# A SwiGLU layer's up passes: the products of the lower right weight blocks, gate and up together, by seven products of half blocks instead of two whole ones

## The chip, the cores and the metric

The kernel runs on one core of one Trainium2 chip. The metric is the device time of one execution in microseconds (us). Before the change it is 2227.25 us, the median of 3 runs (2226.83 to 2227.45).

## What is computed

The reference is one decoder layer in float32: x has 1024 tokens of 1024 features.

```python
x = x + 0.5 * swiglu(rms_norm(x, ffn1_norm), ffn1_w_gate, ffn1_w_up, ffn1_w_down)
h = rms_norm(x, mix_norm)
...                                   # two attentions, gates, output projection
x = x + 0.5 * swiglu(rms_norm(x, ffn2_norm), ffn2_w_gate, ffn2_w_up, ffn2_w_down)
x = x + sigmoid(rms_norm(x, ple_norm) @ w_ple_gate) * (p @ w_ple_proj)

def swiglu(h, w_gate, w_up, w_down):
    return (silu(h @ w_gate) * (h @ w_up)) @ w_down
```

The change lies in the two `swiglu` calls, in `h @ w_gate` and `h @ w_up`: 1024 tokens by 1024 features by 2816 hidden units, each.

## The kernel before

**Products of one block.** The hidden units of gate and up are taken in 22 blocks of 256: block n is a gate block if n is even and an up block if n is odd, so that n = 2j and n = 2j+1 belong together. A block is a product of a 256 x 1024 weight matrix with the 1024 x 1024 activations. `ffn` (L400) does it by a scheme with seven block products in place of eight: both matrices are cut in four, sums of quarters are formed, and seven products of a 128 x 512 weight part with a 512 x 512 part of the activations are added up in four results. They are numbered 1 to 7 in the code. Each number is worked out three times with float32r operands, split in a high part and the rest (high by high, rest by high, high by rest), four slices of 128 deep: 12 matmuls of 128x512, recorded at L584 in `product`. Product 4 is the lower right weight quarter, `part(n, 4)`, against `B[4]`.

**Leaf products.** For products with the same right hand side, the weight parts of two neighbouring blocks can be laid on each other and the scheme can be used once more, at half the size: two products of 128 x 512 by 512 x 512 become seven of 128 x 256 by 256 x 256. The kernel does so for product 2 (`B[2]`) of the blocks n-1 and n, for odd n from 7 to 19. `inner_product` (L525) is one such half product: 6 matmuls of 128x256, recorded at L544, and one addition of the result to the block's sum in SBUF by VectorE (L548; 128x256, one input in PSUM, one in SBUF). The sums of weight halves are made by `inner_sums` (four VectorE additions, L506 to L509, both inputs in SBUF), the sums of the activations once per FFN by `inner_operands`, and kept in four tiles (G, WH, KH, KL) for all blocks.

**Operands.** `prep(n, m)` (L561) makes the left operand of one product: ScalarE copies the high part (L112, a cast), VectorE subtracts for the rest (L113). It stands four steps ahead of the product (`LA = 4`). `sums(n)` makes the sums of a block's weights and `last_sum` another one, both on GpSimd (L475 to L477, L480). `load` fetches a block's weights, two transfers on SyncE's queue, which all transfers share.

**Results.** `evict` moves results out of PSUM: copies on ScalarE (L602, L604, L606), additions on VectorE (L607, L611), SiLU on ScalarE (L614, L616), the products of gate and up on VectorE (L622, L624, L627). Product 4 of a gate block is read from PSUM by the SiLU (L616), that of an up block by the multiplication (L624). `hidden_sums` then forms sums of finished blocks on GpSimd (`block_sums`, L281: four additions, L283 to L286), which go to DRAM for the down product.

**Order.** The order is written out by hand: `seqn` lists the steps (block, product) in the order of TensorE, `seqp` the order in which operands are made. Each engine works through its own queue in the order in which the code records it; a queue does not pass a waiting instruction. A string as product, as in `(n, "65")`, stands for half products.

Of the kernel before, what the change touches and what calls it, by code (L numbers as in the profile page):

```python
# [38 lines left out]
def tile_hybrid_decoder_layer(  # L39
# [131 lines left out]
    fd = dp.tile([NH, S], F32, name="forget_sums")  # L171
    ad = [dp.tile([NF, P, 7, 512], F32, name=f"hidden_{i}") for i in range(2)]
# [227 lines left out]
    def ffn(N, wg, wu, wd, next_gain, resid, hid, tags, entry, tail):  # L400
# [12 lines left out]
        inner = range(6, nm_ - 2)  # L413
        for n in range(4, nm_ - 1):
            if n not in inner:
                steps = [(n, 1), (n - 1, 4), (n, 2), (n - 1, 3), (n, 6), (n, 5), (n, 7)]
                ahead = steps
            elif n % 2 == 0:
                steps = [(n, 1), (n - 1, 4), (n - 1, 3), (n, 6), (n, 5), (n, 7)]
                ahead = steps  # L420
            else:
                steps = [(n, 1), (n - 1, 4), (n, "12"), (n - 1, 3), (n, "65"), (n, 6), (n, "7"), (n, 5), (n, "3"), (n, 7), (n, "4")]
                ahead = [(n, 1), (n, "12"), (n - 1, 4), (n, "65"), (n - 1, 3), (n, 6), (n, "73"), (n, 5), (n, 7), (n, "4"), None]
            seqn += steps
            seqp += ahead
        n = nm_ - 1
        steps = [(n, 1), (n - 1, 4), (n, 2), (n, 6), (n, 5), (n, 7), (n - 1, 3), (n, 3), (n, 4)]
# [5 lines left out]
        turns = {"hl": 0, "t": 0}  # L433
# [18 lines left out]
        def plain(f_, half, parts=(0, 1), out=True):  # L452
# [5 lines left out]
            for kh in parts:  # L458
                hl, rb = hls[0, ((1, 2), (5, 4))[f_][kh]], B[("12", 3)[kh]] if half else N[0]["B"][kh]
# [22 lines left out]
        I = {}  # L482

        def inner_operands(step):

            x_ = I["x"] if step else I.setdefault("x", [slot(t, [P, 2, 512]) for t in ("GF", "RN")])
            a, b = slice(0, 256), slice(256, 512)
            if step < 2:
                nc.vector.tensor_add(x_[step][:], f(pair(2, 0, step)), f(pair(2, 1, step)))
            elif step == 2:  # L490
                nc.vector.tensor_sub(x_[0][:, :, a], x_[0][:, :, b], x_[0][:, :, a])
                nc.vector.tensor_sub(x_[0][:, :, b], x_[1][:, :, b], x_[0][:, :, b])
            elif step == 3:
                nc.vector.tensor_sub(x_[1][:, :, b], x_[1][:, :, b], x_[0][:, :, a])
                nc.vector.tensor_sub(x_[1][:, :, a], x_[1][:, :, a], x_[1][:, :, b])
            else:
                i = step - 4
                t = I[i] = [slot(t, [P, 2, 512], F32R) for t in (("G", "WH"), ("KH", "KL"))[i]]
                split(t[0][:], t[1][:], x_[i][:], nc.scalar, nc.vector)

        def inner_sums(n):

            s = I["s"] = slot("GF", [P, 4, 2, P])
            g, u = part(n - 1, 2), part(n, 2)
# [6 lines left out]
        def inner_prep(n, q):  # L511
            if q == "12":
                inner_sums(n)
                of = part(n - 1, 2)
            elif q == "4":
                of = part(n, 2)[:, 2:4]
# [4 lines left out]
            tag = "RN" if q == "73" else hl_tag()  # L521
            hl = slot(tag, [P, 2, nk, P], F32R)
            split(hl[:, 0], hl[:, 1], of, nc.scalar, nc.vector)
            for i, c in enumerate(q):
                I[c] = hl[:, :, 2 * i:2 * i + 2, :]  # L525
            if q == "12":
                last_sum(n - 1)
            elif q == "4":
                last_sum(n)

        def inner_product(n, c):

# [1290 lines left out]
```

## Time and profile before

| | before |
|---|---|
| median of 3 runs | 2227.25 us |
| the profiled execution | 2226.93 us |
| its span, first to last instruction | 2225.2 us |
| TensorE busy | 2211.6 us, 99% |
| VectorE busy | 1606.7 us, 72% |
| ScalarE busy | 983.6 us, 44% |
| GpSimd busy | 829.0 us, 37% |
| TensorE clock granted | 1.00 |
| first and last half product (L544) | at 163.0 and at 1877.1 us |

The profile is one execution recorded by the hardware. A row of a grouped view names line, engine, operation, output and inputs, then count, busy time, mean duration of one in ns, and the idle time in front of it with what ended it. A matmul's recorded duration overlaps with the next, so the pace of TensorE is read from the starts, not from the duration. The chain of waits is followed back from the last instruction; where it stays on one engine, that engine never waited.

### The profile page before, as it was taken

How to read it: one execution, taken by the hardware profiler on the slowest of the kernel's cores; microseconds unless marked ns; L12 is line 12 of the kernel's file. 1: busy time of each engine (PE TensorE's matmuls, PEld its weight loads, DVE VectorE, ACT ScalarE, POOL GpSimd, SP SyncE). 2: the span in 40 equal slices, each digit the busy share in tenths (PEclk: the TensorE clock that was granted, in tenths of full speed). 3: DMA queues.
4: the chain of work that ended last, by engine and by line, in shares of the span. 5: the costliest groups of instructions: out<-in, count | busy, mean ns of one | idle time of the engine just before them, and what ended most of it. 6: DMA issues, size and time to landing. Idle time of an engine off the chain costs nothing.

```text
span 2225.2 us, 29609 instructions
## 1 busy us (share of the span) xinstructions
PE 2211.6 (99%) x10949; PEld 1860.4 (84%) x10949; DVE 1606.7 (72%) x2390; ACT 983.6 (44%) x1726; POOL 829.0 (37%) x709
## 2 busy tenths in 40 slices
PE   9999999999999999999999999999999999999999
PEld 7888888888889888888988888887888888888887
DVE  7976667597895565666667676799876766778873
ACT  6433333333454555555456564255333333434441
POOL 0344545310015466455456654400644535200111
PEclk9999999999999999999999999999999999999999
DMA  8232323374433133042124246741423332756132
GB/s 323 92 121 88 117 89 123 138 295 145 148 132 94 31 95 93 24 104 72 38 72 119 62 128 213 263 142 54 142 101 103 105 109 92 259 192 211 59 120 89
DMA packets 187713, 278.06 MB, mean 125 GB/s; under 512 B 27944, under 2 KB 110120, under 8 KB 187568
## 3 DMA queue, kind: packets, MB, share of 16 engines
q1 hardware_dynamic: 187568, 276.17, 37.5%
q8 instruction: 86, 1.41, 0.3%
q14 instruction: 59, 0.48, 0.1%
HBM read 192.47 MB, written 75.27 MB: 120 GB/s over the span
## 4 chain that ended last, share of the span: by engine, by line
PE 90%; DVE 5%; ACT 3%; issue 1%; DMA 1%; POOL 0%; SPq 0%; ACTq 0%; DVEq 0%; POOLq 0%
PE ps L584 32%; PE ps L388 19%; PE ps L857 10%; PE ps L849 7%; PE ps L1759 4%; PE ps L1404 3%; PE ps L544 3%; PE ps L1160 3%; PE ps L1136 2%; PE ps L462 2%; PE ps L1085 1%; PE ps L1084 1%; PE ps L1454 1%; DVE H L113 1%; DVE RN L1060 1%
## 5 line engine op out<-in xcount | busy, mean ns | idle before, releaser
L388 PE MATMUL ps<-H,H 128*128 128x512 f32 x2184 | 497.2, 389 | 0.0
L388 PEld LDWEIGHTS ps<-H,H 128*128 128x128 f32 x2184 | 409.5, 188 | 84.8
L584 PE MATMUL ps<-H,WL 128*128 128x512 f32 x816 | 194.7, 390 | 0.0
L584 PEld LDWEIGHTS ps<-H,WL 128*128 128x128 f32 x816 | 151.8, 188 | 30.6
L857 PE MATMUL ps<-H,WH 128*128 128x512 f32 x640 | 175.9, 401 | 0.0
L1139 DVE TENSOR_TENSOR PT<-ps,PT 128x512 fp32r<-128x512 f32 (+1 forms) x160 | 100.6, 634 | 73.2 <-ACT PT L1138 72.2
L396 DVE SCALAR_TENSOR_TENSOR X<-ps,X 128x512 f32<-128x512 f32 x168 | 108.7, 685 | 41.8 <-PE ps L388 41.7
L584 PE MATMUL ps<-H,Q 128*128 128x512 f32 x552 | 132.8, 390 | 0.0
L857 PEld LDWEIGHTS ps<-H,WH 128*128 128x128 f32 x640 | 113.9, 188 | 19.0
L1138 ACT CAST PT<-ps 128x512 fp32r<-128x512 f32 (+1 forms) x160 | 86.9, 549 | 83.5 <-PE ps L1136 79.4
L146 POOL TENSOR_TENSOR WL<-RAW,WH 128x512 fp32r<-128x512 f32 (+1 forms) x92 | 109.1, 1206 | 38.6 <-ACT WH L136 33.0
L584 PE MATMUL ps<-X,WL 128*128 128x512 f32 x504 | 121.5, 390 | 0.0
L584 PEld LDWEIGHTS ps<-H,Q 128*128 128x128 f32 x552 | 102.4, 188 | 20.4
L480 POOL TENSOR_TENSOR KL<-KL,RAW 128x512 f32<-128x512 f32 x20 | 26.1, 1303 | 242.4 <-DVE Q L113 100.2
L209 POOL TENSOR_TENSOR PT<-PT,RN 128x1024 f32<-128x1024 f32 x2 | 4.8, 2402 | 295.1 <-ACT RN L203 295.1
L849 PE MATMUL ps<-WH,H 128*128 128x256 f32 (+2 forms) x576 | 111.4, 323 | 0.1
L584 PEld LDWEIGHTS ps<-X,WL 128*128 128x128 f32 x504 | 93.9, 188 | 19.6 <-DVE WL L113 0.5
L1097 POOL TENSOR_TENSOR T<-T,l 128x128 f32<-128x128 f32 (+3 forms) x64 | 73.1, 1148 | 88.7 <-DVE l L1096 84.7
L1160 PE MATMUL ps<-PT,X 128*128 128x256 f32 (+1 forms) x480 | 101.2, 315 | 3.9 <-DVE PT L1139 2.3
L1160 PEld LDWEIGHTS ps<-PT,X 128*128 128x128 f32 x480 | 76.7, 189 | 22.7 <-DVE PT L1139 9.7
L1107 POOL TENSOR_TENSOR T<-T,RN 128x383 f32<-128x383 f32 (+2 forms) x64 | 77.1, 1205 | 46.0 <-DVE RN L1060 43.7
L1060 DVE TENSOR_TENSOR_SCAN RN<-GF,RN 128x127 f32<-128x127 f32 (+2 forms) x96 | 91.1, 949 | 2.7
(468 smaller groups left out, 5116.9 us busy)
## 6 DMA issues: line engine op xcount, KB each, us to landing
hidden<-PT SPq DMA_DIRECT2D x40, 512.0 KB, 2.9
WH<-in_ffn_w_gate_dram SPq DMA_DIRECT2D x38, 512.0 KB, 4.3
Q<-hidden SPq DMA_DIRECT2D x24, 512.0 KB, 6.8
hidden<-RN SPq DMA_DIRECT2D x22, 512.0 KB, 2.6
KH<-in_ffn_w_up_dram SPq DMA_DIRECT2D x20, 512.0 KB, 3.8
KL<-in_ffn_w_up_dram SPq DMA_DIRECT2D x20, 512.0 KB, 3.8
T<-in_ffn_w_down_dram SPq DMA_DIRECT2D x20, 512.0 KB, 4.6
RAW<-in_w_in_dram SPq DMA_DIRECT2D x18, 512.0 KB, 4.3
```

Source lines behind the costliest of these rows:

```text
L146: ins = eng_lo.tensor_sub(lo[part], raw[part], f(hi[part]))
L388: pe(nc.tensor.matmul(groups[g][t][:], wt[:, b, k, t * P:(t + 1) * P], act[:, a, k, :], start=(fresh and n == 0), stop=(i in (6, 1, 4) and ...
L396: nc.vector.scalar_tensor_tensor(xs, groups[g][t][:], scale, xs, ALU.mult, ALU.add)
L584: pe(nc.tensor.matmul(ps[:], hl[:, a, k, :], rhs(m, b, k), start=(first and i == 0), stop=(final and i == 11), skip_group_check=True))
L849: pe(nc.tensor.matmul(ps[:, :n], hT[t // 4][a][:, k, (t % 4) * P:(t % 4 + 1) * P], w[k // d][b][:, k % d, :n], start=(i == 0), stop=(i == ...
L857: pe(nc.tensor.matmul(ps[:], w[a][:, k, :], hT[half][b][:, k, :], start=(i == 0), stop=(i == 23)))
L1060: order("dve", nc.vector.tensor_tensor_scan(*args))
L1107: nc.gpsimd.tensor_mul(T[:, cut:n - 1], T[:, cut:n - 1], R[:, cut:n - 1])
L1138: high = nc.scalar.copy(pt[:, 0, :width], ps[:, :width])
L1139: low = nc.vector.tensor_sub(pt[:, 1, :width], ps[:, :width], f(pt[:, 0, :width]))
L1160: pe(nc.tensor.matmul(o, lh, r, start=(kpair == c and i == 0), stop=(kpair == 0 and i == len(mm) - 1)))
L1759: pe(nc.tensor.matmul(ps, pl["w"][d, k // 2][b][:, k % 2, m * P:(m + 1) * P], hT[half][a][:, k, cs], start=(i == 0), stop=(i == 23)))
```

## The change

Product 4 of two neighbouring blocks is now done by seven half products too, in pairs that are shifted by one: an up block n-1 and the next gate block n, for even n from 8 to 20. So `inner` holds all n from 7 to 20; odd n take `part(.., 2)` and `B[2]`, even n `part(.., 4)` and `B[4]` (`leaf_of`).

- In each of the two FFNs 14 whole products (12 matmuls of 128x512 each) go, and 7 x 7 half products (6 matmuls of 128x256 each) come. The steps of a pair of blocks are reordered, and `seqp` is now the same as `seqn`.
- The half products of a gate block add to E[n][1] after ScalarE has copied product 7 there as well (L679, a second copy); the SiLU of that half (L598) and the product of gate and up (L601) read SBUF, behind these additions, and no longer PSUM.
- The sums of the activations are needed twice now and do not fit. `inner_tile` makes four tiles for each of the two; those of half product 5 stay in SBUF, those of 6, 7 and 4 are written to DRAM (6 transfers of 512 KB per FFN) and fetched again for each use (`inner_load`, 42 transfers of 512 KB per FFN, two tiles ahead, in one KL and one WH buffer that alternate).
- Buffers for left operands are handed out from a list of free ones (`hl_slot`).
- The block sums on GpSimd of a finished pair now follow the step `(n, "34")` of an even n.

Line numbers shift: what is L548 before is L594 after, L550 is L596, L616 L598 (in SBUF) or L689, L624 L601 (in SBUF) or L697, L607 L680, L611 L684, L480 L489, L283 to L286 L284 to L287.

The core of the diff:

```diff
-        inner = range(6, nm_ - 2)
+        inner = [n for n in range(6, nm_ - 1) if n > 6 and (n % 2 == 0 or n < nm_ - 2)]
+        by_inner = {2: [m for n in inner if n % 2 for m in (n - 1, n)], 4: [m for n in inner if n % 2 == 0 for m in (n - 1, n)]}
         for n in range(4, nm_ - 1):
...
+            steps = [(n, 1)]
+            if n - 1 in inner and n % 2:
+                steps.append((n - 1, "34"))
...
+            elif n % 2:
+                steps += [(n, "65"), (n, 6), (n, "7"), (n, 5), (n, 7), (n, "34")]
             else:
...
+                steps += [(n, "6"), (n, 6), (n, 5), (n, 7), (n, "57")]
             seqn += steps
-            seqp += ahead
+            seqp += steps
...
+        def inner_tile(leaf, c):
+
+            i, cs = {"5": (0, 0), "7": (0, 256), "4": (1, 0), "6": (1, 256)}[c]
+            t = slot("WH" if c != "5" else ("G", "KH")[leaf // 4], [P, 2, 2, 256], F32R)
+            split(t[:, 0], t[:, 1], I["x"][i][:, :, cs:cs + 256], nc.scalar, nc.vector)
+            if c == "5":
+                TT[leaf, c] = t
+            else:
+                nc.sync.dma_start(td[leaf, c], f(t[:]))
...
+        def inner_load():
+
+            n, c = stream[turns["s"]]
+            t = TT[n, c] = slot(("KL", "WH")[turns["s"] % 2], [P, 2, 2, 256], F32R)
+            nc.sync.dma_start(f(t[:]), td[leaf_of(n), c])
+            turns["s"] += 1
...
+            nc.vector.tensor_add(to, to, ps)
+            if m == 2 and c == "3":
+                nc.scalar.activation(x1[:], x1[:], AF.Silu)
+            elif m == 4 and c == "4":
+                nc.scalar.activation(y1[:, 0, :], y1[:, 0, :], AF.Silu)
+            elif m == 4 and c == "3":
+                g2 = E[n - 2][1]
+                nc.vector.tensor_mul(g2[:, 0, :], g2[:, 0, :], x1[:, 0, :])
+                nc.sync.dma_start(hid[(n - 2) // 2, :, 1:3, :], g2[:])
+            if c in "674" and turns["s"] < len(stream):
+                inner_load()
...
+        INNER_AT = {x_: (2 + 2 * (i // 6), i % 6) for i, x_ in enumerate(((4, 1), (3, 4), (4, 2), (3, 3), (4, 6), (4, 7), (5, 1), (4, 4), (5, 2), (4, 3), (5, 6), (5, 7)))}
...
             elif m == 7:
                 nc.scalar.copy(e2[:, 1, :], ps[:])
+                if n in by_inner[4]:
+                    nc.scalar.copy(e2[:, 0, :], ps[:])
...
+                if n % 2 == 0 and n in inner and m == "34":
+                    hidden_sums(n - 1, ("PT", "PT"))
+                elif n % 2 and m == (4 if n == 1 else 3) and n < nm_ - 1 and n not in by_inner[4]:
                     hidden_sums(n, ("PT", "PT"))
```

The steps of a pair of blocks, an even n and the odd n+1, in TensorE's order, before: (n, 1), (n-1, 4), (n-1, 3), (n, 6), (n, 5), (n, 7), (n+1, 1), (n, 4), (n+1, "12"), (n, 3), (n+1, "65"), (n+1, 6), (n+1, "7"), (n+1, 5), (n+1, "3"), (n+1, 7), (n+1, "4"). After: (n, 1), (n, "12"), (n-1, 3), (n, "6"), (n, 6), (n, 5), (n, 7), (n, "57"), (n+1, 1), (n, "34"), (n+1, "12"), (n, 3), (n+1, "65"), (n+1, 6), (n+1, "7"), (n+1, 5), (n+1, 7), (n+1, "34").

Three places show what moves on the engines beside TensorE. In these rows a number behind a tile's name is its buffer's; GF and RN hold the two halves of a gate block, Y those of an up block, PT the sums of finished blocks, WL, Q and PT left operands.

The first is ScalarE and VectorE in an up block, around the SiLU of the gate's second half. ScalarE before:

```order
L614 ACTIVATE RN_1519<-RN_1519 128x512
L112 CAST WL_1624<-GF_1584 128x512
L602 COPY Y_1640<-ps_1627 128x512
L112 CAST WL_1643<-WH_1347 128x512
L616 ACTIVATE RN_1519<-ps_1505 128x512
L112 CAST Q_1663<-RAW_1556 128x512
```

ScalarE after:

```order
L687 ACTIVATE RN_1929<-RN_1929 128x512
L112 CAST WL_2040<-WH_1712 128x512
L112 CAST Q_2060<-WH_1712 128x512
L673 COPY Y_2080<-ps_2067 128x512
L112 CAST Q_2083<-GF_2035 128x512
L598 ACTIVATE RN_1929<-RN_1929 128x512
L112 CAST PT_2105<-RAW_1996 128x512
```

The SiLU of one half of RN (L616, L598) reads PSUM before and SBUF after; behind it on the queue stands the high part of the up block's product 6 (Q_1663 before, PT_2105 after). VectorE at the same place, from the operand of "12" on, before:

```order
L113 TENSOR_TENSOR PT_1589<-WH_1347,PT_1589 128x512
L113 TENSOR_TENSOR WL_1606<-WH_1347,WL_1606 128x512
L607 TENSOR_TENSOR RN_1519<-RN_1519,ps_1593 128x512
L113 TENSOR_TENSOR WL_1624<-GF_1584,WL_1624 128x512
L113 TENSOR_TENSOR WL_1643<-WH_1347,WL_1643 128x512
L113 TENSOR_TENSOR Q_1663<-RAW_1556,Q_1663 128x512
```

VectorE after:

```order
L113 TENSOR_TENSOR WL_2040<-WH_1712,WL_2040 128x512
L594 TENSOR_TENSOR RN_1929<-RN_1929,ps_1942 128x256
L594 TENSOR_TENSOR RN_1929<-RN_1929,ps_1934 128x256
L113 TENSOR_TENSOR Q_2060<-WH_1712,Q_2060 128x512
L113 TENSOR_TENSOR Q_2083<-GF_2035,Q_2083 128x512
L594 TENSOR_TENSOR Y_1729<-Y_1729,ps_1942 128x256
L601 TENSOR_TENSOR RN_1577<-RN_1577,Y_1729 128x512
L594 TENSOR_TENSOR RN_1929<-RN_1929,ps_1934 128x256
L113 TENSOR_TENSOR PT_2105<-RAW_1996,PT_2105 128x512
```

The last addition to RN_1929, which the SiLU of L598 reads, stands behind two operands (Q_2060, Q_2083) and the product of gate and up of the blocks before (L601). `inner_sums` of the up block stand ahead of the first row.

The second is GpSimd in the same pair of blocks. Before:

```order
L283 TENSOR_TENSOR PT_1863<-GF_1518,RN_1519 128x512
L284 TENSOR_TENSOR PT_1863<-PT_1863,GF_1518 128x512
L285 TENSOR_TENSOR PT_1864<-GF_1518 128x512
L286 TENSOR_TENSOR PT_1864<-RN_1519,PT_1863 128x512
L480 TENSOR_TENSOR WH_1647<-WH_1647,RAW_1755 128x4x128
L480 TENSOR_TENSOR KL_1792<-KL_1792,RAW_1856 128x4x128
```

After:

```order
L489 TENSOR_TENSOR WH_1712<-WH_1712,RAW_1844 128x4x128
L284 TENSOR_TENSOR PT_2108<-GF_1576,RN_1577 128x512
L285 TENSOR_TENSOR PT_2108<-PT_2108,GF_1576 128x512
L286 TENSOR_TENSOR PT_2109<-GF_1576 128x512
L287 TENSOR_TENSOR PT_2109<-RN_1577,PT_2108 128x512
L489 TENSOR_TENSOR KL_1892<-KL_1892,RAW_1996 128x4x128
```

The four sums of finished blocks stood ahead of the gate's last sum (WH) and stand behind it now.

The third is ScalarE at the turn from an up block to the next gate block, around the SiLU of the tile GF (both halves, 128x1024). Before:

```order
L550 ACTIVATE GF_1518<-GF_1518 128x1024
L112 CAST WL_1770<-KL_1492 128x512
L606 COPY Y_1641<-ps_1627 128x512
L112 CAST Q_1788<-KL_1492 128x512
L112 CAST Q_1802<-RAW_1755 128x512
```

After:

```order
L112 CAST WL_2240<-KL_1892 128x512
L596 ACTIVATE GF_1928<-GF_1928 128x1024
L112 CAST WL_2264<-GF_2216 128x512
L673 COPY GF_2280<-ps_2267 128x512
L112 CAST WL_2283<-RAW_2196 128x512
```

The cast behind the SiLU was one of a whole product's operand (WL_1770, product 4) and is now that of half product "6" of the gate block (WL_2264).

More of the change, by code (lines that the diff above doesn't have):

```diff
@@ L171, in tile_hybrid_decoder_layer @@
     fd = dp.tile([NH, S], F32, name="forget_sums")
+    td_ = [dp.tile([P, 2, 2, 256], F32, name=f"inner_{i}") for i in range(12)]
     ad = [dp.tile([NF, P, 7, 512], F32, name=f"hidden_{i}") for i in range(2)]
@@ L432, in ffn @@
         W, hls, E = {}, {}, {}
-        turns = {"hl": 0, "t": 0}
+        turns = {"hl": 0, "t": 0, "s": 0}
         def cyc(key, tags):
@@ L458, in plain @@
             for kh in parts:
-                hl, rb = hls[0, ((1, 2), (5, 4))[f_][kh]], B[("12", 3)[kh]] if half else N[0]["B"][kh]
+                hl, rb = hls[0, ((1, 2), (5, 4))[f_][kh]][0], B[("12", 3)[kh]] if half else N[0]["B"][kh]
                 for a, b in ((0, 0), (1, 0), (0, 1)):
@@ L496, in inner_operands, with leaf_of @@
             else:
-                i = step - 4
-                t = I[i] = [slot(t, [P, 2, 512], F32R) for t in (("G", "WH"), ("KH", "KL"))[i]]
-                split(t[0][:], t[1][:], x_[i][:], nc.scalar, nc.vector)
+                inner_tile(leaf, "6574"[step - 2])
+                if step == 5:
+                    del I["x"]
+        stream = [(n, c) for n in inner for c in "674"]
+        def inner_load():
[3 more added lines that the diff above has]
+            turns["s"] += 1
+        def leaf_of(n):
+            return 2 if n % 2 else 4
         def inner_sums(n):
+            m = leaf_of(n)
             s = I["s"] = slot("GF", [P, 4, 2, P])
-            g, u = part(n - 1, 2), part(n, 2)
+            g, u = part(n - 1, m), part(n, m)
             lo, hi = slice(0, 2), slice(2, 4)
@@ L545, in inner_product, with hl_slot @@
                     i += 1
-            g1, u1 = E[n - 1][0], E[n][0]
-            for to in {"1": (g1[:, 0, a],), "2": (g1[:, 0, a],), "6": (g1[:, 0, b],), "5": (u1[:, 0, b],), "7": (u1[:, 0, b],), "3": (g1[:, 0, b],), "4": (u1[:, 0, a],)}[c]:
-                nc.vector.tensor_add(to, to, ps)
-            if c == "3":
-                nc.scalar.activation(g1[:], g1[:], AF.Silu)
-        def hl_tag():
+            uses[0] -= 1
+            if uses[0] == 0:
+                free.append(uses[1])
+            x1, y1 = (E[k][m // 4] for k in (n - 1, n))
+            to = {"1": x1[:, 0, a], "2": x1[:, 0, a], "6": x1[:, 0, b], "5": y1[:, 0, b], "7": y1[:, 0, b], "3": x1[:, 0, b], "4": y1[:, 0, a]}[c]
+            nc.vector.tensor_add(to, to, ps)
[9 more added lines that the diff above has]
+                inner_load()
+        free = []
+        def hl_slot(nk=4):
             k = turns["hl"]
             turns["hl"] += 1
-            return tags["hl"][k] if k < len(tags["hl"]) else ("WL", "WL", "WL", "Q", "Q", "PT")[k % 6]
+            if k < len(tags["hl"]):
+                tag = tags["hl"][k]
+            else:
+                if k == len(tags["hl"]):
+                    held = [t for (i, _), (_, t) in hls.items() if i]
+                    for t in ("WL", "WL", "WL", "Q", "Q", "PT"):
+                        if t in held:
+                            held.remove(t)
+                        else:
+                            free.append(t)
+                    assert not held, held
+                tag = free.pop(0)
+            return slot(tag, [P, 2, nk, P], F32R), tag
         def prep(n, m):
@@ L563, in prep @@
                     last_sum(n)
-            hl = hls[n, m] = slot(hl_tag(), [P, 2, 4, P], F32R)
+            hls[n, m] = hl_slot()
+            hl = hls[n, m][0]
             split(hl[:, 0], hl[:, 1], part(n, m), nc.scalar, nc.vector)
@@ L579, in product @@
             first, final = m in (1, 2, 5), m in (4, 2, 3)
-            hl = hls.pop((n, m))
+            hl, tag = hls.pop((n, m))
+            if turns["hl"] > len(tags["hl"]):
+                free.append(tag)
             i = 0
@@ L616, in evict @@
                     nc.scalar.activation(e2[:, 0, :], ps[:], AF.Silu)
-                elif m == 3 and n not in inner:
+                elif m == 3 and n not in by_inner[2]:
                     nc.scalar.activation(e1[:], e1[:], AF.Silu)
```

74 lines of the change are left out of this document (43 added, 31 removed).

## The prediction

> **What bounds the kernel now.** First the page's busy times, then what TensorE waited for (the waits, TensorE alone), then three pairs of blocks as windows, then the chain of waits inside one pair.
>
> ```profile
> PE 2211.6 (99%) x10949; PEld 1860.4 (84%) x10949; DVE 1606.7 (72%) x2390; ACT 983.6 (44%) x1726; POOL 829.0 (37%) x709
> ...
> PE ps L1160 <- DVE PT L1139: 2.3, 9, 0.5
> ...
> PE ps L584 <- DVE PT L113: 0.2, 1, 0.2
> ```
>
> TensorE is busy 99% of the span; its longest kind of wait is 2.3 us in all, and the whole products (L584) waited 0.2 us once. TensorE is the bound, and everything else is hidden behind it.
>
> ```profile
> core 0: us, PE busy (x) PEld busy (x) DVE busy (x) ACT busy (x) POOL busy (x), PEclk, DMA share, GB/s
> ...
> 238.99:276.77 37.78, 37.78 (x188) 32.05 (x188) 25.62 (x34) 13.78 (x25) 17.74 (x12) 1.00 0.32 105
> ...
> 201.21 1.43 PE ps L544 x12
> 202.64 2.75 PE ps L584 x12
> 205.39 1.43 PE ps L544 x12
> 206.82 2.75 PE ps L584 x12
> 209.57 0.71 PE ps L544 x6
> ...
> 217.20 21.79 PE ps L584 x96
> 238.99 1.43 PE ps L544 x12
> ```
>
> A pair of blocks takes 37.78 us, all of it TensorE, at the full clock; VectorE works 25.6 us of it in 34 instructions, GpSimd 17.7. The chain stays on TensorE and gives its prices: a whole matmul 21.79/96 = 0.2270 us (a product 2.72), one of a half product 1.43/12 = 0.1192, and about 0.03 each time that whole products follow halves (2.75 against 2.72).
>
> **TensorE's own gain.** Per FFN 14 whole products of 12 go: 2 x 14 x 12 = 336 matmuls, 336 x 0.2270 = 76.3 us. 2 x 49 half products of 6 come: 588 x 0.1192 = 70.1 us. Runs of halves go from 5 to 7 per pair, 28 more changes at 0.03, 0.8 us. Together -5.4 us: seven half-size products for two whole ones (eight halves' worth) save little here because a half matmul costs 0.525 of a whole one. With the row 0.71/6 in place of 1.43/12 the term is -5.9.
>
> [...]
>
> So the whole gain is a quarter of a per cent, 0.4 us per pair, and it is there only if the other engines stay hidden. I count a change within 0.2% (4.5 us) as none, about what a measurement of this kernel can tell.
>
> **What VectorE gets.** Its prices, from the groups of the three pairs:
>
> ```profile
> L548 DVE TENSOR_TENSOR GF<-GF,ps 128x256 f32<-128x256 f32 x12 | 5.0, 418 | 3.0 <-PE ps L544 2.7
> L506 DVE TENSOR_TENSOR GF<-WH,KL 128x256 f32<-128x256 f32 x3 | 4.5, 1514 | 0.0
> ...
> L622 DVE TENSOR_TENSOR RN<-RN,Y 128x512 f32<-128x512 f32 x3 | 3.2, 1075 | 0.1
> L624 DVE TENSOR_TENSOR RN<-RN,ps 128x512 f32<-128x512 f32 x3 | 2.1, 688 | 2.7 <-PE ps L584 2.7
> ...
> L113 DVE TENSOR_TENSOR Q<-KH,Q 128x512 fp32r<-128x512 f32 x3 | 2.0, 683 | 0.0
> ...
> L480 POOL TENSOR_TENSOR KL<-KL,RAW 128x512 f32<-128x512 f32 x3 | 3.9, 1286 | 37.6 <-DVE WL L113 25.1 <-DVE Q L113 12.5
> ```
>
> Per pair come 7 additions of half products (7 x 0.42 = 2.9 us), one and a half operands (1.0) and 4 sums of weight halves; the product L624 becomes one with both inputs in SBUF (0 to 0.4 more). The sums are the open price: no row shows one undisturbed, so 0.42 us (as L548, the same size) is the low end and 1.51 (L506) the high end, 1.7 to 6.1 us for four. VectorE goes from 25.6 us to between 31.2 and 36.0 of a pair that should take 37.4. On average it still fits. It works in order, though, so what counts is whether each operand is ready when TensorE comes to it.
>
> L506 costs 1.51 us because GpSimd is adding at the same time:
>
> ```profile
> 211.03 1.28 POOL L480 TENSOR_TENSOR KL<-KL,RAW 128x512 f32<-128x512 f32 x1 [12.53 <-DVE WL L113]
> 211.20 1.67 DVE L113 TENSOR_TENSOR WL<-WH,WL 128x512 fp32r<-128x512 f32 x1
> 212.28 1.74 POOL L475 TENSOR_TENSOR RAW<-WH 128x512 f32<-128x512 f32 x1
> ...
> 227.73 1.62 POOL L283 TENSOR_TENSOR PT<-GF,RN 128x512 f32<-128x512 f32 x1 [1.22 <-issue]
> 228.12 1.51 DVE L506 TENSOR_TENSOR GF<-WH,KL 128x256 f32<-128x256 f32 x1
> ```
>
> A VectorE operation with both inputs in SBUF that starts during a GpSimd addition ends 0.56 us after it (212.87 against 212.31), and the next GpSimd addition ends 1.15 us after that (214.02): the two take turns, 1.7 us a turn. Additions with one input in PSUM are not held up (L548, L624).
>
> **Wait A: product 6 of an up block.** I set t = 0 at the start of product 1 of an up block n. By the prices above TensorE comes to product 6 at t = 2.75 + 4 x 0.71 + 2.75 + 2 x 0.71 = 9.8. Its high part (PT_2105) stands on ScalarE behind the new SiLU in SBUF (L598), and that waits for VectorE's last addition to RN. The pieces on ScalarE:
>
> ```profile
> 235.06 0.68 DVE L607 TENSOR_TENSOR RN<-RN,ps 128x512 f32<-128x512 f32 x1
> ...
> L604 ACT COPY Y<-ps 128x512 f32<-128x512 f32 x3 | 1.8, 586 | 17.1 <-PE ps L584 17.1
> ...
> 235.76 0.64 ACT L614 ACTIVATE RN<-RN 128x512 f32<-128x512 f32 x1 [1.59 <-DVE RN L607]
> 236.30 0.60 ACT L112 CAST Q<-GF 128x512 fp32r<-128x512 f32 x1
> ```
>
> Product 7 of the gate block ends at -1.4. Then: copy 0.6 to -0.8, addition 0.68 to -0.1, four sums 1.6 (undisturbed: GpSimd is idle there) to 1.5, operand of "12" 0.68 to 2.1, GpSimd's last sum 1.28, which waits for it, to 3.5, cast of Q_2060 0.6 to 4.1. Now the sums of finished blocks, which stood ahead of that last sum before, run behind it from 3.5. So Q_2060 is held up by the first to 5.4, Q_2083 by the second (to 6.5) to 7.1, L601 by the third (to 8.2) to 8.8; the addition to RN ends at 9.1, the SiLU lets the queue go on at 9.7, the cast ends at 10.3: 0.55 us late. Without the turns the cast would end at 8.5, in time. With one more turn it would be some 1.1 late, taking 0.6 off the slack elsewhere. Six up blocks per FFN (9 to 19) have this neighbourhood: 12 x 0.55 = 6.6 us, bounds 0 and 13.
>
> **Wait B: half product "6" of a gate block.** GpSimd makes the weight sums of the next two blocks from about t = 15 on, when the operand of "34" has released the last sum ahead of them, just when VectorE makes the four inner sums: four turns like L506's, to about 23, and the operand of "12" ends at 23.5, just in time for 23.45 + 0.24 (two matmuls need only the high part). Behind it stand L680, L695 and the operand of product 3 (3 x 0.65, to 25.5) and the addition for "3" (25.8). The SiLU of GF waits for that:
>
> ```profile
> 214.23 1.06 ACT L550 ACTIVATE GF<-GF 128x1024 f32<-128x1024 f32 x1 [3.22 <-DVE GF L548]
> ```
>
> It ends at 26.9, the cast behind it at 27.4, the rest on VectorE at 28.1. With wait A in the pair, TensorE needs it at 27.6 + 0.24: 0.25 late undisturbed, 0.9 with one more turn (GpSimd's last two sums fall there). I take 0.6, and six gate blocks per FFN: 12 x 0.6 = 7.2 us. The low end is 0; the high end 1.6, if product 3's operand loses a turn as well (0.75 more), so 0 to 19 us.
>
> **The set-up.** VectorE makes the activation sums twice, and the first lot moves ahead to where it is fullest:
>
> ```profile
> 97.50:119.20 21.70, 21.70 (x97) 17.97 (x96) 20.54 (x18) 7.23 (x13) 18.35 (x12) 1.00 0.44 158
> ...
> 109.96 1.18 DVE L113 TENSOR_TENSOR Q<-WH,Q 128x512 fp32r<-128x512 f32 x1
> ...
> 116.97 2.32 DVE L489 TENSOR_TENSOR GF<-H 128x1024 f32<-128x1024 f32 x1
> ...
> 126.70 0.68 DVE L491 TENSOR_TENSOR GF<-GF 128x512 f32<-128x512 f32 x1
> ```
>
> Two sums (2.3 each) and four differences (0.68, or 1.7 with turns) go in ahead of the operand at 109.96, whose product starts about 117.0: 7.3 to 11.4 us against a slack of 117.9 - 111.1 = 6.8 and 1 us of idle time: 0 to 3.6 late, I take 1.0 per FFN, 2.0 in all. The second lot falls where the only one lay before and costs nothing more there. ScalarE's second copy (0.59 per block) is free as well: ScalarE works 13.8 of 37.8 us. Its bounds are 0 and the 0.5 us by which it delays the SiLU behind it, which nobody waits for.
>
> **The reloads.** 84 fetches and 12 writes of 512 KB.
>
> ```profile
> WH<-in_ffn_w_gate_dram SPq DMA_DIRECT2D x38, 512.0 KB, 4.3
> ```
>
> A fetch starts when TensorE has left the tile two before; by the steps, the shortest time from there to its use is 8.3 us ("4" of a gate block to "7" of the next up block). With 4.3 us to land, 4 us are spare. On SyncE's queue the fetch for "4" of an up block stands behind the stores of GpSimd's block sums (about t = 10) and is used at 19.4. The store behind L601 comes some steps later than it did behind L624; the next reader of those halves is GpSimd, counted in A. I count nothing.
>
> **The sum.** -5.4 + 6.6 + 7.2 + 2.0 = +10.4 us. The profiled execution took 2226.9 us (0.3 less than the median, span 2225.2 and 1.7 around it): 2237.3 there, 2237.6 beside the median.
>
> **Rivals.** *VectorE keeps up* (faster). If GpSimd's additions start later than I have them, by a buffer that is still held, the turns fall elsewhere and both waits vanish: -5.4 us, 2221.9. For: no wait in the trace of before, where VectorE has 12 us to spare in each pair; A turns on 0.55 us in a chain of 11. It decides if that chain loses one turn of 1.7. Against: the chain is new, and the turns are in every pair of the trace. 0.17.
>
> *One wait only* (no change). A alone: -5.4 + 6.6 = +1.2, 2228.5; B alone: +1.8. B falls away if the next up block's weights land 1 us later, since GpSimd's sums then start after the SiLU. 0.21.
>
> *Reloads late* (slower by more). The DMA share of 0.32 rises by 6 x 512 KB per pair, from 105 to some 190 GB/s. If a fetch takes over 8.3 us to land, one tile per pair is late: at 2 us, 14 x 2 - 5.4 = +22.6, 2249.9. Against: 4.3 us now. 0.10.
>
> **How the numbers follow.** The forecast, both waits, has 0.52; its own range is 2230 to 2250 (all three waits at half their size: -5.4 + 7.9; and half way to their upper ends: -5.4 + 9.9 + 13.2 + 4.6), 0.04 of it within 0.2% of now. Faster 0.17, no change 0.21 + 0.04 = 0.25, slower 0.48 + 0.10 = 0.58. The range reaches down to the case in which VectorE keeps up and up to the forecast's upper end: 2221 to 2251.
>
> **What would show it.** Right: pairs of 38 to 39.5 us instead of 37.4; TensorE waiting for ScalarE's cast (L112) at product 6 of up blocks and at "6" of gate blocks, L598 and L596 waiting for VectorE, VectorE busy 31 to 36 us a pair with GpSimd additions of 1.7 us beside it. Wrong: pairs of 37.4 us with no wait on TensorE, or waits for DMA in front of half products.

## The result, and the profile after

The changed kernel takes 2314.74 us (median of 5 runs, 2314.24 to 2315.89), the kernel before 2227.25 us (2226.80 to 2227.98, 5 runs): a ratio of 1.0393, 95% interval 1.0378 to 1.0409. It is slower, as forecast, but by 87.5 us where the forecast had 10.4.

From the page of the changed kernel, and then from its waits, TensorE alone (what waited, for what; us in total, times, the longest):

```profile
PE 2235.0 (97%) x11201; PEld 1879.3 (81%) x11201; DVE 1713.5 (74%) x2596; ACT 1013.9 (44%) x1794; POOL 821.7 (36%) x709
```

```profile
PE ps L587 <- ACT WL L112: 29.3, 12, 3.0
PE ps L587 <- ACT PT L112: 15.5, 6, 3.0
PE ps L655 <- ACT Y L675: 7.8, 2, 4.4
PE ps L587 <- ACT Q L112: 7.6, 6, 1.3
PE ps L655 <- DVE WL L113: 2.5, 3, 2.1
```

The span grew from 2225.2 to 2312.5 us. TensorE is idle 63.9 us more (77.5 against 13.6) and busy 23.4 us more, although it was given less work. Where: the windows of the two up passes, before,

```profile
29.74:449.49 419.75, 419.75 (x1990) 352.67 (x1988) 308.14 (x380) 164.02 (x282) 169.13 (x113) 1.00 0.35 119
1508.20:1920.80 412.60, 412.39 (x1954) 345.77 (x1952) 302.31 (x371) 159.50 (x274) 169.39 (x113) 1.00 0.32 105
```

and after (length; busy PE, PEld, DVE, ACT, POOL; granted clock; DMA share; GB/s):

```profile
29.82:492.25 462.43, 430.46 (x2116) 361.60 (x2115) 360.46 (x482) 178.59 (x315) 165.96 (x113) 0.98 0.48 162
1551.38:2007.80 456.42, 424.33 (x2080) 356.00 (x2078) 355.74 (x474) 174.45 (x308) 166.29 (x113) 0.97 0.45 150
```

The up passes lost 42.7 and 43.8 us, 86.5 of the 87.3. VectorE is busy 78% of them, so it has room on average, and the granted clock is below 1. Inside one pair, the timeline of TensorE:

```profile
279.76 2.91 PE L655 MATMUL ps<-T,WL 128*128 128x512 f32 x12
283.97 0.95 PE L587 MATMUL ps<-WH,WL 128*128 128x256 f32 x6 [1.30 <-ACT Q L112]
...
294.38 2.91 PE L655 MATMUL ps<-H,WL 128*128 128x512 f32 x12
...
300.00 2.91 PE L655 MATMUL ps<-T,Q 128*128 128x512 f32 x12
305.94 1.01 PE L587 MATMUL ps<-KL,WL 128*128 128x256 f32 x6 [3.03 <-ACT WL L112]
306.75 1.49 PE L587 MATMUL ps<-G,WL 128*128 128x256 f32 x6
308.04 3.88 PE L655 MATMUL ps<-H,WL 128*128 128x512 f32 x12
311.75 0.88 PE L587 MATMUL ps<-WH,PT 128*128 128x256 f32 x6
```

Product 3 at 300.00 is through at 302.7 (12 x 0.227), and the next half product, "6" of the up block's "65", begins at 305.94: 3.2 us of nothing. Half product "6" of the gate block waits 1.5 us (282.5 to 283.97). Both come 12 times. What follows the longer wait is stretched too: the six matmuls at 306.75 take 1.49 where such a group takes 0.88, the twelve at 308.04 take 3.88 where the same takes 2.91.

What TensorE waits for at 305.94, in the timeline of the same stretch, all engines:

```profile
298.70 1.12 DVE L113 TENSOR_TENSOR Q<-WH,Q 128x512 fp32r<-128x512 f32 x1 [1.20 <-ACT Q L112]
299.35 1.62 POOL L285 TENSOR_TENSOR PT<-PT,GF 128x512 f32<-128x512 f32 x1
299.74 1.78 DVE L113 TENSOR_TENSOR WL<-GF,WL 128x512 fp32r<-128x512 f32 x1
300.94 1.73 POOL L286 TENSOR_TENSOR PT<-GF 128x512 f32<-128x512 f32 x1
301.44 0.41 DVE L594 TENSOR_TENSOR Y<-Y,ps 128x256 f32<-128x256 f32 x1
301.89 1.34 DVE L601 TENSOR_TENSOR RN<-RN,Y 128x512 f32<-128x512 f32 x1
303.15 0.41 DVE L594 TENSOR_TENSOR RN<-RN,ps 128x256 f32<-128x256 f32 x1
303.65 0.63 ACT L598 ACTIVATE RN<-RN 128x512 f32<-128x512 f32 x1 [3.97 <-DVE RN L594]
304.18 0.60 ACT L112 CAST WL<-RAW 128x512 fp32r<-128x512 f32 x1
304.82 0.69 DVE L113 TENSOR_TENSOR WL<-RAW,WL 128x512 fp32r<-128x512 f32 x1 [1.26 <-ACT WL L112]
305.43 0.94 DVE L594 TENSOR_TENSOR GF<-GF,ps 128x256 f32<-128x256 f32 x2
```

The operand of "65" (WL from GF) was ready at 301.5. What comes 0.1 us before TensorE's restart is the end of the first of the two additions at 305.43 (305.43 + 0.41): the eviction of half product "1". Half product "6" adds to the same bank, so it can't begin before that. The eviction stands in VectorE's queue behind the split of product 6's operand; this waits for ScalarE's cast, the cast stands behind the SiLU L598, and the SiLU waits for VectorE's eviction of half product "4". All of this is a single chain, and ahead of it three VectorE operations with both inputs in SBUF (298.70, 299.74, 301.89) are longer than 0.68 us beside GpSimd's block sums. The profile names a cast of ScalarE (L112) as the releaser; half product "6" waits for several semaphores, and the cast of its own operand had ended at 299.7. In all 24 waits of this trace the restart comes 0.10 us behind the end of such an eviction. It does so too in the next run, where ScalarE's last cast had ended 0.3 us and more before.

The clock, as windows on both sides of 306.7:

```profile
303.30:306.70 3.40, 0.76 (x6) 0.79 (x7) 2.03 (x5) 2.70 (x5) 1.26 (x1) 1.00 0.83 201
306.70:310.10 3.40, 3.40 (x13) 2.99 (x12) 2.73 (x6) 0.00 (x0) 0.00 (x0) 0.50 0.97 392
310.10:313.50 3.40, 3.40 (x19) 2.88 (x18) 0.62 (x2) 1.55 (x4) 0.12 (x1) 1.00 0.46 183
```

Behind a stretch in which TensorE worked 0.76 of 3.40 us, it runs at 0.50 for one window of 3.41 us: 13 matmuls in it against 19 in the next. The trace has 13 such windows in the up passes. 10 of them stand behind a wait of 3.2 us, 9 of the 12 waits in all, since one was followed by two; the other 3 stand behind waits in the set-up of the passes.

### The profile page after: what moved, and what is told of

The parts are those of the page before. It is cut to its first block, busy times and chain, and to the rows that moved or that the text cites. A ratio compares the mean times of both kernels' runs of the same rounds, so it can differ in the third digit from the quotient of the medians.

```text
span 2312.5 us, 30613 instructions
## 1 busy us (share of the span) xinstructions
PE 2235.0 (97%) x11201; PEld 1879.3 (81%) x11201; DVE 1713.5 (74%) x2596; ACT 1013.9 (44%) x1794; POOL 821.7 (36%) x709
## 5 line engine op out<-in xcount | busy, mean ns | idle before, releaser
L655 PE MATMUL ps<-H,WL 128*128 128x512 f32 x888 | 221.6, 401 | 2.5 <-DVE WL L113 2.5
L655 PEld LDWEIGHTS ps<-H,WL 128*128 128x128 f32 x888 | 169.7, 196 | 37.9 <-DVE WL L113 4.0
L655 PE MATMUL ps<-H,PT 128*128 128x512 f32 x432 | 105.6, 396 | 0.2 <-DVE PT L113 0.2
L489 POOL TENSOR_TENSOR KL<-KL,RAW 128x512 f32<-128x512 f32 x20 | 26.1, 1306 | 209.5 <-DVE Q L113 90.8
L655 PEld LDWEIGHTS ps<-H,PT 128*128 128x128 f32 x432 | 81.6, 192 | 17.8 <-DVE PT L113 1.3
L934 PE MATMUL ps<-H,WL 128*128 128x512 f32 x320 | 91.6, 399 | 0.0
L926 PEld LDWEIGHTS ps<-WH,H 128*128 128x128 f32 x576 | 84.6, 189 | 6.7 <-PE ps L926 0.3
```

The source lines that it names most:

```text
L655: pe(nc.tensor.matmul(ps[:], hl[:, a, k, :], rhs(m, b, k), start=(first and i == 0), stop=(final and i == 11), skip_group_check=True))
L926: pe(nc.tensor.matmul(ps[:, :n], hT[t // 4][a][:, k, (t % 4) * P:(t % 4 + 1) * P], w[k // d][b][:, k % d, :n], start=(i == 0), stop=(i == ...
L934: pe(nc.tensor.matmul(ps[:], w[a][:, k, :], hT[half][b][:, k, :], start=(i == 0), stop=(i == 23)))
```

## The experiments

My theory after the traces was that the waits come from the order of the queues: SiLUs that wait hold casts, these hold splits, and these the eviction of "1". The rivals were late reloads, GpSimd's sums, which stretch VectorE's operations, and a cost of the clock of its own. Each variant but the best one was run once, beside the kernel before on the same chip (2227.0 to 2227.9).

**The SiLUs later.** `late` is a list of calls that is worked off behind the preparations of step "12".

```diff
-                nc.scalar.activation(x1[:], x1[:], AF.Silu)
+                late.append(lambda: nc.scalar.activation(x1[:], x1[:], AF.Silu))
...
-                nc.scalar.activation(y1[:, 0, :], y1[:, 0, :], AF.Silu)
+                late.append(lambda: nc.scalar.activation(y1[:, 0, :], y1[:, 0, :], AF.Silu))
```

> Against the changed kernel (2314.74 us), the two silus behind the half products (lines 596 and 598) are issued later: after the casts of the next steps' operands, at the end of step "12", instead of straight behind the eviction they need. Nothing else changes. Theory (silus in ScalarE's queue hold the casts, these VectorE's splits, and these the eviction whose bank half product "6" waits for): the wait before "65" of the up blocks (3.19 us, 12 times) falls by about 1.3 to some 1.9 us, since the split no longer waits for silu and cast; the wait before "6" of the gate blocks (1.45 us, 12 times) falls below 0.3. That is 12 x 1.3 + 12 x 1.2 = 30 us, and with shorter waits most of the half-clock stretches behind them should go, 10 to 17 us more: about 2270 us (2260 to 2287). Rival, the reloads are late: waits unchanged, 2312 to 2317. Rival, VectorE simply has too much work: it is no less busy, so at most 5 us less.

2299.42 us, 15.3 less: a third of the 45 that the theory gave, and outside its range. The wait before "65" fell only to 2.9 us. The same place in its timeline:

```profile
299.37 1.73 POOL L286 TENSOR_TENSOR PT<-GF 128x512 f32<-128x512 f32 x1
...
301.58 0.41 DVE L594 TENSOR_TENSOR RN<-RN,ps 128x256 f32<-128x256 f32 x1
301.80 1.27 POOL L287 TENSOR_TENSOR PT<-RN,PT 128x512 f32<-128x512 f32 x1 [0.69 <-DVE RN L601]
301.91 1.70 DVE L113 TENSOR_TENSOR WL<-RAW,WL 128x512 fp32r<-128x512 f32 x1
...
303.54 0.93 DVE L594 TENSOR_TENSOR GF<-GF,ps 128x256 f32<-128x256 f32 x2
```

The split no longer waits for the SiLU and starts at once, and then takes 1.70 us instead of 0.69, because it now runs beside GpSimd's last block sum, as it did not before. The SiLU and its cast had covered that: 1.26 us of waiting went and 1.01 us of contention came. In these rows the split of 1.70 us ends 0.54 us after the block sum beside which it began. The additions of L594, with one input in PSUM, show no such stretch: in the changed kernel's trace the 43 that lie wholly within GpSimd's work take 0.41 to 0.42 us and the 99 clear of it 0.40 to 0.42, where the splits (L113, 128x512, both inputs in SBUF) take 1.01 to 1.80 us within it (45 of them) and 0.68 to 0.70 clear of it (277).

**No reloads.** Half products "6", "7" and "4" read the resident tile of "5"; stores and loads go.

```diff
-                t = TT[leaf_of(n), c] if c == "5" else TT.pop((n, c))
+                t = TT[leaf_of(n), "5"]
...
-            if c in "674" and turns["s"] < len(stream):
-                inner_load()
```

> Against the changed kernel (2314.74 us), the right-hand tiles of half products "6", "7" and "4" are neither stored nor reloaded; these half products read the resident tile of "5" instead, so their values differ (that part of the computation is changed). 12 stores and 84 reloads of 512 KB are gone, all else stays. Theory (VectorE's and ScalarE's queues): the waits stay, 2308 to 2316 us. Rival, the reloads are late or crowd the transfers: the waits before "65" and "6", 56 us in all, go, and the half-clock stretches with them: about 2240 us.

2342.51 us: 27.8 slower, which neither had. So the reloads are not late. The waits here name the evictions themselves (line 594 is 592 here):

```profile
PE ps L585 <- DVE GF L592: 36.8, 12, 3.1
PE ps L585 <- DVE Y L592: 23.6, 12, 2.0
```

The wait of the gate blocks grew to 2.1 us. Its timeline ahead of that wait,

```profile
282.34 1.35 POOL L485 TENSOR_TENSOR KH<-KH,KL 128x512 f32<-128x512 f32 x1
282.47 1.78 DVE L113 TENSOR_TENSOR PT<-KL,PT 128x512 fp32r<-128x512 f32 x1
```

and the same two operations in the changed kernel:

```profile
277.09 0.68 DVE L113 TENSOR_TENSOR PT<-KL,PT 128x512 fp32r<-128x512 f32 x1
...
279.72 1.30 POOL L485 TENSOR_TENSOR KH<-KH,KL 128x512 f32<-128x512 f32 x1 [2.83 <-DMA KL<-in_ffn_w_up_dram]
```

In the changed kernel the second half of the raw up weights goes into a buffer that a reloaded tile still holds; its fetch is issued 6.5 us behind that of the first half, and 0.4 us behind it in this run. GpSimd's sums wait for it there and miss VectorE's split. Without reloads GpSimd goes on without a pause, and the split takes 1.78 us. That is 1.1 us more per pair, 0.4 in front of half product "12" and 0.7 in front of "6", some 13 us over 12 pairs. The half-clock windows rose from 13 to 19, at up to 1.7 us each (half of 3.41), and the granted clock fell from 0.990 to 0.986. These two make most of the 27.8 us; the rest was not traced.

**The wait filled.** 14 matmuls of no use in front of "65".

```diff
+            if m == 3 and n in by_inner[4] and n + 1 in by_inner[2] and n % 2 == 0:
+                extra = bank_of[n + 1, "d"] = bank("pf")
+                for i in range(14):
+                    pe(nc.tensor.matmul(extra[:], hl[:, i % 2, i % 4, :], rhs(m, 0, i % 4), start=(i == 0), stop=(i == 13), skip_group_check=True))
```

> Against the changed kernel (2314.74 us), 14 extra matmuls of 128x512 (3.2 us by 0.227 each) stand in TensorE's queue in front of every "65" of the up blocks, where it now waits 3.19 us; their result is dropped, in a bank that is free there. Theory (the stretches of half clock follow from the idle time of this wait): the waits for VectorE stay where they are, but TensorE is busy in them, so the 10 half-clock windows of 3.41 us behind them go, at half of 3.41 us each: 17 us less, about 2298 us (2294 to 2304), with a granted clock near 1.00 in the passes, though TensorE has 168 matmuls more to do. Rival, the half clock costs nothing of its own or comes from something else: 2314 us or a little more. Rival, the extra matmuls delay the chain they hide in: up to 2320 us.

2300.16 us, 14.6 less with 168 more matmuls, within the theory's range. No half-clock window is left in the pairs (four are left in the set-up), and the granted clock is 0.997, where the changed kernel had 0.990. So this part of the loss is the clock's, and the waits only cause it.

**No block sums on GpSimd.**

```diff
-            block_sums(hid[j], *E[n - 1], tags)
+            if tags[0] == "PT":
+                for i in range(2):
+                    nc.sync.dma_start(hid[j, :, 3 + 2 * i:5 + 2 * i, :], E[n - 1][1 - i][:])
+            else:
+                block_sums(hid[j], *E[n - 1], tags)
```

> Against the changed kernel (2314.74 us), GpSimd's four block sums per pair (lines 284 to 287) are left out of the up passes; the gate and up blocks are stored in their place, as many bytes, so the down passes read other values. Theory, contention part (VectorE's operations take 1.1, 1.8 and 1.3 us beside these sums where 0.68 is the usual time, all on the chain before "65"): the wait before "65" falls from 3.19 by about 2.1 to 1.1 us, 12 times 2.1 = 25 us, and the half-clock stretches behind it go, 15 us more: about 2274 us (2262 to 2290). Rival, only the order of the queues matters: less than 8 us. Rival, reloads are late: no change.

2262.30 us, 52.4 less, at a granted clock of 1.00. The chain before "65":

```profile
285.71 0.69 DVE L113 TENSOR_TENSOR WL<-GF,WL 128x512 fp32r<-128x512 f32 x1 [0.31 <-ACT WL L112]
...
286.77 0.69 DVE L601 TENSOR_TENSOR RN<-RN,Y 128x512 f32<-128x512 f32 x1
...
289.67 0.94 DVE L594 TENSOR_TENSOR GF<-GF,ps 128x256 f32<-128x256 f32 x2
...
290.19 0.59 PE L587 MATMUL ps<-KL,WL 128*128 128x256 f32 x3 [1.25 <-ACT WL L112]
```

All operations are back at 0.69 us, and the wait is 1.4 us (product 3 was through at 288.75): 1.8 us of the 3.2 were contention. 12 x 1.8 = 21 us, the clock 19, and the rest in the set-up. The gate blocks' wait stayed at 1.4 us.

**Evictions first.** The operands of the step three behind "12" are prepared behind its evictions.

```diff
-                if s + LA < len(seqn):
-                    prep(*seqp[s + LA])
+                ahead = LA - (s + 1 < len(seqn) and seqn[s + 1][1] == "12")
+                while done < min(s + ahead, len(seqn) - 1):
+                    done += 1
+                    prep(*seqp[done])
```

> Against the changed kernel (2314.74 us), one thing is moved: the operands of the step three after each "12" are cast and split behind the evictions of "12" (line 594) and no longer ahead of them, so the eviction whose bank "6" waits for has one split fewer in front of it. Theory (the place of the evictions in VectorE's queue): before "65" of the up blocks the eviction can follow the one of "4", which ended 1.9 us earlier, so 3.19 falls to about 1.3; before "6" of the gate blocks one split of 0.68 goes, so 1.45 falls to about 0.8. That is 12 x 1.9 + 12 x 0.65 = 31 us and most of the 22 us of half clock: about 2267 us (2258 to 2285). Rival, beside GpSimd's sums whatever stands in the queue is stretched, and the gain is eaten as with the late silus: 2295 to 2305 us.

2276.58 us, 38.2 less, within the theory's range: 3.2 fell to 1.2 us, 1.5 to 0.9 or less, and the half clock behind them went (granted clock 0.998); new waits of 0.4 to 1.6 us before half product "7" took some of it. TensorE again restarts 0.1 us behind the end of the first of the two additions:

```profile
298.57 0.93 DVE L594 TENSOR_TENSOR GF<-GF,ps 128x256 f32<-128x256 f32 x2
...
299.08 0.95 PE L587 MATMUL ps<-KL,WL 128*128 128x256 f32 x6 [1.07 <-issue]
```

The place of one eviction behind one split was worth more than the SiLUs.

**Late SiLUs and no block sums.**

> The late silus and the left-out block sums of GpSimd together (the same part of the down passes' inputs is replaced as in the run without block sums, 2262.30 us). There, the wait before "65" was 1.41 us, and the silu with the cast behind it (1.27 us) stood in its chain. Theory (two causes in one chain: queue order and GpSimd): now both waits are nearly gone, the first to below 0.3, the second to 0.3 from 1.42: about 2262.3 - 12 x 1.2 - 12 x 1.1 = 2235 us (2229 to 2244). Rival, the sums of the raw weights on GpSimd still stretch VectorE's splits before "6": that wait stays near 1.0 as with the late silus alone, 2243 to 2249 us. Rival, the silus never mattered: 2260 us.

2245.19 us. The wait before "65" is gone. The one before "6" of the gate blocks is still 1.1 to 1.6 us in 8 of 12 pairs: the rival's case. New waits of 0.4 to 1.1 us stand before half product "7" in 10 of the pairs, which neither had. There the sums of the raw weights stretch both splits ahead of the eviction:

```profile
264.51 1.30 POOL L485 TENSOR_TENSOR KH<-KH,KL 128x512 f32<-128x512 f32 x1 [3.16 <-DMA KL<-in_ffn_w_up_dram]
264.74 1.62 DVE L113 TENSOR_TENSOR WL<-GF,WL 128x512 fp32r<-128x512 f32 x1
...
266.28 1.78 DVE L113 TENSOR_TENSOR WL<-RAW,WL 128x512 fp32r<-128x512 f32 x1
267.99 0.94 DVE L594 TENSOR_TENSOR Y<-Y,ps 128x256 f32<-128x256 f32 x2
```

**Everything late.** Late SiLUs, evictions first, and the product L601, its store and the block sums behind step "12" as well.

```diff
+                def finish():
+                    nc.vector.tensor_mul(g2[:, 0, :], g2[:, 0, :], x1[:, 0, :])
+                    nc.sync.dma_start(hid[(n - 2) // 2, :, 1:3, :], g2[:])
+                    hidden_sums(n - 1, ("PT", "PT"))
+
+                late.append(finish)
```

> Against the changed kernel (2314.74 us): late silus, evictions of "12" first, and the product with the neighbour (line 601), its store and GpSimd's block sums also behind the evictions of "12". Everything is still computed. Theory: the chain before "65" is then two splits and four evictions, which end before TensorE has done product 3, so both waits go (56 us) and with them the half clock (22 us): about 2240 us (2234 to 2256), with what is left in the set-up, some 12 us of waits. Rival, the block sums moved behind "12" stretch the evictions of the next products, which then hold TensorE: 2260 to 2290 us.

2250.72 us, 64.0 less than the changed kernel with the same work, within the theory's range. A pair, as a window, and what TensorE still waits for in the passes:

```profile
257.13:294.96 37.83, 37.67 (x204) 32.39 (x205) 31.68 (x48) 15.61 (x30) 17.82 (x12) 1.00 0.56 188
```

```profile
PE ps L661 <- ACT Y L681: 9.4, 2, 4.9
...
PE ps L587 <- issue: 2.0, 12, 0.2
```

A pair takes 37.83 us with 0.33 of waiting in it by the starts (0.2 in the view, which counts from the modelled ends): 37.50 without, 0.28 less than the 37.78 of before. That is TensorE's whole gain, and the set-up's two long waits, 9.4 us in the view, outweigh it; shorter waits there and the half clock behind them (granted clock 0.997) come on top.

**The block sums on VectorE.** `hidden_sums` is given nc.vector.

> As the run with everything late, and the four block sums of each pair are on VectorE (0.69 us each by the uncontended rows) and no longer on GpSimd. Theory (GpSimd's sums cost VectorE more than the sums would cost on VectorE itself): VectorE's operations fall back to 0.69 us, no wait is left in the pairs, 2228 to 2240 us, and below the run with everything late. Rival, VectorE has no room for 2.8 us more behind "12": the eviction of product 3 comes late and TensorE waits up to 2.8 us a pair, 34 us above that run.

2255.17 us: 4.4 slower than on GpSimd. The theory fails, and the rival's wait comes at a third of its size: VectorE's operations at that place are back at 0.68 us, but the four sums stand ahead of the evictions of product 3 and of "6", and half product "7" of the up blocks now waits 0.95 us (9.4 us over 12 in the view).

**The second leaf's operands later, and the late block placed three ways.** First, with everything late, leaf 4's operands are made five steps later:

```diff
-(5, 1), (4, 4), (5, 2), (4, 3), (5, 6), (5, 7)
+(5, 5), (5, 7), (6, 1), (5, 4), (5, 3), (6, 6)
```

> As the run with everything late (2250.72 us), and the operands of leaf 4 (their four sums, four splits and stores) are made in the steps from product 5 of block 5 to product 6 of block 6, five steps later than now. Theory (the set-up: the copy of product 6 of block 5 stands on ScalarE behind a silu, and that behind VectorE's sums and splits for leaf 4, stretched by GpSimd): the waits of 1.1 and 4.6 us there in FFN1, 1.1 and 5.1 us in FFN2, go, and the half clock behind them, 4 us by the two records: 12 + 4 = 16 us less, about 2235 us (2231 to 2243). Rival, the work is only moved and stretches the next evictions as much: 2246 to 2256 us.

2237.61 us, 13.1 less; the two long waits for ScalarE's copy in the set-up are gone. Then `finish` behind product 6 of the up block (by the code three steps behind "12", where the expectation says two):

> As the run with everything late and leaf 4 spread, and the product with the neighbour (line 601), its store and the block sums stand behind product 6 of the up block, two steps later than there. Theory: the wait of 0.33 us that is left before half product "7" of the up blocks (12 times) goes, since the eviction of "6" has no product by the neighbour ahead of it: 4 us below that run, about 2231 us. Rival, the block sums then meet the raw weights' sums on GpSimd and VectorE's operand sums get longer: equal or up to 20 us above it.

2262.45 us, the rival's case. GpSimd's block sums now stand directly ahead of the raw weights' sums, and eight sums without a pause lie beside VectorE's operand sums; its splits end late, and products wait for them 0.7 and 1.2 us in every pair. Then one step ahead of that place (the expectation says two), behind the evictions of "65":

> As the run with everything late and leaf 4 spread (2237.61 us), and the product with the neighbour (line 603 there), its store and the block sums stand one step behind the evictions of "65", that is behind the eviction of "6" that half product "7" waits 0.32 us for, and two steps ahead of the place of the second variant (2262.45 us). Theory: the 0.32 us before "7" go (12 times, 3.8 us), and GpSimd's last block sum still ends before its sums of the raw weights are due, so nothing else moves: about 2234 us (2231 to 2237), still some 6 us above the kernel before, since TensorE's own gain is small and the set-up's waits stay. Rival, GpSimd's queue: its last block sum waits for the later product, the raw weights' sum behind it comes later, and the cast of its result holds VectorE's splits as in the second variant: 2242 to 2262 us.

2232.32 us (2231.45 to 2233.57): 1.0024 of the kernel before, 95% interval 1.0014 to 1.0033. It is the best version of the change and still some 5 us slower than the kernel without it: its pairs take 37.50 us with no wait, and some 8 us of waits around the set-up of the two passes outweigh that gain.

**Everything late, without reloads**, against the odd loss above:

> As the run with everything late (2250.72 us), without stores and reloads of the inner tiles: half products "6", "7" and "4" read the resident tile of "5" (that part of the computation is changed). It settles the loss of 28 us that leaving out the reloads brought before. Theory (the reloads only set when the raw up weights arrive and with that when GpSimd's sums run beside VectorE; they cost nothing themselves): with the waits gone there is little to shift, 2247 to 2254 us. Rival, the reloads do help or cost by themselves: more than 6 us away from 2250.7 us.

2255.38 us, 4.7 above the same kernel with reloads: 1.4 outside the theory's range and short of the rival's 6. With the waits gone the 28 us have shrunk to 5, 3.0 of them in the first up pass and 1.2 in the second. So the reloads are no cost; what is left of the loss is not traced to its place.

## Why the prediction was right and wrong

The direction was right, and both waits were named, wait B at its place and wait A two half products behind the place where it came. The size was not right: the range ended at 2251.

| step | predicted us | measured us |
|---|---|---|
| TensorE's own gain | -5.4 | -3.4 (12 pairs at 37.50 for 37.78) |
| wait A, now in front of "65" of the up blocks | 6.6 (0 to 13) | 38 (12 x 3.2) |
| wait B, "6" of the gate blocks | 7.2 (0 to 19) | 18 (12 x 1.5) |
| set-up | 2.0 (0 to 7.2) | 15 |
| half clock behind the waits | not in the sum | 19 |
| reloads | 0 | no cost found |

The waits, the set-up and the half clock are summed from the starts of the matmuls in the changed kernel's trace (what a matmul took beyond 0.227 or 0.119 us). The column adds up to 87, as measured, to within 1.5. TensorE's own gain came out 2 us smaller: by an estimate from the paces of 0.2270 and 0.1192 us, the seven changes from half to whole products in a pair cost 0.25 us together, and the five of before 0.08.

**Wait A: the step that failed** is that TensorE comes to product 6 at t = 9.8, taken as the time by which the chain must be through. The chain itself came as forecast. With product 1 of the up block at 294.38, the SiLU ended at t = 9.9 (forecast 9.7) and the cast behind it at 10.4 (10.3). But TensorE comes to "65" before it comes to product 6, at 8.3 (302.7), and "65" needs the bank of "1" evicted, and that eviction stands behind the split of product 6's operand. So to the 0.55 us belong 1.43 (two half products earlier), 0.6 (the split) and 0.5 (the eviction and its signal): 3.1 us, and 3.2 was measured. I had followed each operand to its product, and no eviction to the next half product that writes its bank; the run with the evictions first, which takes that split from in front of the eviction, won 38 us. Wait B has the same flaw: the forecast put the split of "6" 0.25 to 0.9 us late and left out the split of product 6 (0.6) and the eviction (0.5) behind them.

**The set-up** failed at "the second lot falls where the only one lay before and costs nothing more there". The lots follow each other without a gap, and the second meets GpSimd's sums of the next weights. There, too, it is an eviction: ScalarE's copy L675 of product 6, behind a SiLU and two casts.

```profile
137.53 1.81 DVE L518 TENSOR_TENSOR RN<-RN 128x512 f32<-128x512 f32 x1
139.27 1.75 DVE L113 TENSOR_TENSOR WL<-KH,WL 128x512 fp32r<-128x512 f32 x1
...
143.94 1.06 ACT L691 ACTIVATE GF<-GF 128x1024 f32<-128x1024 f32 x1 [5.22 <-DVE GF L684]
...
145.93 0.57 ACT L675 COPY Y<-ps 128x512 f32<-128x512 f32 x1
```

Making the second lot five steps later won 13 us.

**The clock** was in no term. In the changed kernel none of the twelve waits of 1.5 us had half clock behind it and nine of the twelve of 3.2 us did, and the half clock cost about half as much again (19 us beside 38). **The reloads** were rightly counted at nothing, and the rival that had them late is refuted. **The turns** of VectorE and GpSimd were seen and priced at 1.7 us each, and the traces agree (1.6 to 1.8 us for most); the mistake was to count them only up to the operand. **VectorE** is busy 31.7 us in a pair (forecast 31 to 36): its total was never the bound.

Not settled: three waits of 0.4 to 0.5 us in each pass, some 3 us in all, which the kernel before does not have. They stand at product 5 of block 4 and products 1 of block 5 and 4 of block 4, right behind the first lot of activation sums, for which the forecast had 2.0. They are gone in the runs without block sums, so contention is in them; moving the work there was not tried.

## What to carry to other kernels

When half the matmuls of a product are taken away and the rest are half as wide (0.71 us for a half product here, 2.72 for a whole one), the time between the last write of a PSUM bank and the next one to it shrinks as well: follow each eviction through its engine's queue to the next matmul on its bank, as carefully as each operand to its product. On a bound engine with 0.3 us to win per pair, an instruction that stands ahead of an eviction and waits for another engine can cost more than the work saved (here 38 us in front of "65" for 3.4 saved). And a queue that waits can hide contention (with the late SiLUs 1.26 us of waiting went and 1.01 of contention came): where a wait is removed, look at what the freed instruction then runs beside.

## What the hardware showed unexpectedly

In the trace of the changed kernel the 11 stretches at half clock inside the execution last 3.41 us (nine) or 6.83 us (two), and the ten at full clock between them 40.96, 68.27, 81.92 or 1218.56 us, which is 12, 20, 24 or 357 times 3.413. Cut into windows of 3.413 us along these edges, this trace has 12 windows at full clock in which TensorE was idle 0.596 of the time or more, and half clock came behind each of them (behind one at the end of the execution); all others were idle 0.50 or less, and it came behind none (windows already at half clock left out). The nine waits of 3.2 us with half clock behind them each made one window idle for 0.60 to 0.89; the three others fell on two windows each, idle 0.38 to 0.50. The twelve waits of 1.5 us had none behind them. Without reloads, where the gate blocks wait 2.1 us, the granted clock was 0.986, against 0.990 with them.

A kernel with 84 fetches of 512 KB fewer was 27.8 us slower, for the most part because weights that arrived earlier moved GpSimd's sums beside VectorE's splits.
